# Eight whole gates in place of twelve behind the second mixer of a hybrid decoder step

## The chip, the cores and the metric

The kernel runs on one core of a Trainium2 chip. The metric is the device time of one execution in microseconds (us); the figure for the kernel before is the median of three runs. A core has five engines with instruction streams of their own: TensorE (PE, with its weight loads shown apart as PEld), VectorE (DVE), ScalarE (ACT), GpSimd (POOL) and SyncE (SP, which here only issues transfers). They wait for one another through semaphores. PE multiplies into eight banks of PSUM; everything else lives in SBUF or in memory (HBM).

## What is computed

One step of a decoder layer for a prompt of 512 tokens and eight samples of one token each, so 520 columns in all. The input is normalised and modulated to h, and one wide projection of h feeds two token mixers that run in parallel, a matrix memory (mLSTM) and a forgetting attention (FoX), and the gates that merge them. A gated MLP with a short convolution follows.

```python
mq, mk, mv, mo, mi, mf, fq, fk, fv, ff, ga, gb = jnp.split(h @ w_in + b_in, SPLIT_POINTS, axis=-1)
...
y_m = mlstm_output(h_m, mo, m_hnorm_w)
q_f = rmsnorm(split_heads(fq, F_HEADS), f_qnorm_w)
k_f = rmsnorm(split_heads(fk, F_HEADS), f_knorm_w)
v_f = split_heads(fv, F_HEADS)
lf_f = jax.nn.log_sigmoid(ff.astype(jnp.float32))
y_f = fox_fn(q_f, k_f, v_f, lf_f)
merged = jax.nn.sigmoid(ga) * (y_m @ w_proj_a) + jax.nn.sigmoid(gb) * (y_f @ w_proj_b)
x = x + g1 * (merged @ w_out)
```

The model width is 2048. FoX has 8 heads of 128. For the prompt it is causal attention with a bias from the forget values, swept in blocks of 128 queries. For the samples the past lies in pages of 128 rows, two pages for each of the eight samples, found through a page table; a page row holds all eight heads.

```python
pk = cache_k[layer, page_table].reshape(DB, P, H, Dh).astype(k.dtype)
pv = cache_v[layer, page_table].reshape(DB, P, H, Dh).astype(v.dtype)
...
s = jnp.einsum('bqhd,bkhd->bhqk', q, k_all).astype(jnp.float32) * scale
s = s + (Fq.transpose(0, 2, 1)[..., :, None] - F.transpose(0, 2, 1)[:, :, None, :])
p = jax.nn.softmax(s, axis=-1).astype(v.dtype)
out = jnp.einsum('bhqk,bkhd->bqhd', p, v_all)
```

## The kernel before

**Tiles and precision.** A weight chunk is 128 rows of 2048 values, in two halves of 128x1024. Every product is made of three: ACT casts the half to a high part (`wh`), DVE subtracts to get the low part (`wl`), and PE multiplies high by high, high by low and low by high. An activation has 520 columns, in two pieces of 260, so one 128x128 block of a weight costs 6 matmuls of 260 columns. The inputs `h` lie as pairs of tiles `hh`, `hl`.

**Gates.** Of the 32 gate chunks (16 `ga`, 16 `gb`), `NG` = 2 are made early. `gates = range(NG, KC + NB2)` is made two by two by `GatePair`, in the loop of pairs (`run_pairs`): a unit of 7 steps, each of 24 matmuls, makes two chunks with 7 products in place of 8 (the products are the tiles `x`, `y` and `z`), and the sums that this asks for are DVE work. Pairs whose chunk belongs to `gb` write it to memory (`dsg`), from where it is fetched for the merge. The remaining `range(NB2, KC)` of `gb`, twelve chunks before, are whole gates: 16 blocks of 6 matmuls each in two `halves`, tile `gate`.

**The second mixer behind the gates.** The last loop before the projection `pb` runs over the 24 halves, and each half has 8 steps of 6 matmuls: 192 steps. Behind each step it runs what `plan` holds for that step, put there by hand with `put(step, f)`. PE, DVE, ACT are in program order from the pair loop on, SP and POOL from its end on, so a step's place in the code is its place on every engine, and a waiting instruction holds up all behind it on its engine. In half n, the weights of half n + 4 are loaded at its step 3 (`gate_load`), and those of half n + 2 are cast at step 2 (`gate_cast`, ACT) and split at step 4 (`gate_low`, DVE).

**Heads.** Head hh starts at b = 1 + 22 hh. Its five inputs are loaded at b − 20 (`f_load`); `f_norm` scales q and k (tiles `fi`, DVE); `f_split`, `f_values` and their low parts make `fqh`, `fkh`, `fvh` (ACT) and `fql`, `fkl`, `fvl` (DVE); `f_scores` for four blocks of queries at b + 8, 9, 11, 12 make `fS` (PE), a step later `f_max` adds the bias and takes the maximum (DVE, tile `fs`) and ACT the exponential, two steps on `f_scale` divides (DVE). At b + 19 to 21 `f_turn` transposes the weights into `fPT` (PE), and `f_turn_low`, two steps later, makes `fpl` (DVE), after which that bank is free. `f_attend` follows at b + 26 to 29. The ring of banks `mm_ps`, for all these PSUM tiles, has four.

**Samples.** Sixteen units of key pages (two pages of the table by one half of the heads; `s_load`) each load one query row `qb` to all partitions and gather two tiles `kp` of 128x512 with an indirect transfer that POOL issues. `s_scores` is a multiplication and a reduction for each tile on DVE. Then come the offsets (`s_offsets`, whose product reads the tile `lfd`), the turn of all scores (`s_turn`, tiles `pqk` and `sS`), the maximum, the weights, and eight `s_attend` (tile `sO`) of four value tiles `vp` each. `y_split` and `y_sample` bring the outputs of prompt and samples together for `pb`.

**Rings.** `st` holds 33 tiles, `pt` 9, `raw` (128x1024, weights) 7, `wh` and `wl` 3 each. A tile is free for its next owner once the last reader of the one before is done; the issuing engine waits for that.

Of the kernel before, what the change touches and what calls it, by code (L numbers as in the profile page):

```python
# [22 lines left out]
NS = 8  # L23
# [4 lines left out]
FH = 8  # L28
# [35 lines left out]
def tile_hybrid_step(ctx: ExitStack, tc: tile.TileContext, I, O):  # L64
    nc = tc.nc
    S, V, G, T, Y = nc.scalar, nc.vector, nc.gpsimd, nc.tensor, nc.sync
# [20 lines left out]
    def mconst(shape, name, dt=F32, tag=None):  # L87
        return cm.tile(shape, dt, tag=tag or name, name=name)
# [16 lines left out]
    def dram(shape, name):  # L105
        return dp.tile(shape, F32, tag=nm(name), name=nm(name))
# [48 lines left out]
    def raw_tile():  # L155
        return wp.tile([P, 1024], F32, tag="raw", name=nm("raw"), bufs=7)
# [18 lines left out]
    def on(f, *a):  # L175
        return lambda: f(*a)
# [416 lines left out]
    h = []  # L593
# [42 lines left out]
    T, V, S = (Ordered(tc, e) for e in (T, V, S))  # L636
# [90 lines left out]
    for i, (c0, n) in enumerate(phases):  # L727
        todo = {j: [] for j in range(NPRE)}

        def put(j, f, *a):  # L730
            todo[j].append(on(f, *a))
# [13 lines left out]
        if i + 1 < len(phases):  # L745
            a, b = range(c0 + n, c0 + 2 * n)
# [86 lines left out]
    T, V, S = nc.tensor, nc.vector, nc.scalar  # L833
# [33 lines left out]
    def gather(dst, src, idx):  # L867
        return G.indirect_dma_start(dst, None, src, bass.IndirectOffsetOnAxis(ap=idx, axis=0))
# [9 lines left out]
    acc, gt, _ = w_in("gates")  # L878
# [338 lines left out]
    H = mheads = follows = None  # L1217
# [40 lines left out]
                G.dma_start(dxf[i + 8 * (n == 4)][:, :N], t[:, :N])  # L1258


    NB2 = 4
    assert (NG + NB2) % 2 == 0
    dsg = dram([KC, P, N], "dsg")

# [172 lines left out]
    def s_load(i):  # L1437

        e, b = divmod(i, NS)
        qb = pt("qb")  # L1440
        Y.dma_start(qb[:, :512], dqf[e, b].partition_broadcast(P))
        kps = [pt("kp") for _ in range(NPG)]
        W.k[i] = qb, kps
        for g, kp in enumerate(kps):
            gather(kp[:, :512], I["cache_k"], idx_h[e][:, b * NPG + g:b * NPG + g + 1])

    class Pages:
        pass

    W = Pages()  # L1450
    W.v, W.k = {}, {}

    root = {}
    dss, drr = dram([2, FH, N], "dss"), dram([2, FH, N], "drr")
# [48 lines left out]
    t0, tq = 7 * (len(units) - 2), 7 * (2 * FH)  # L1503
    halves = [(j, e) for j in range(NB2, KC) for e in range(2)]
    gw = {}

    def gate_load(n):
        if n < len(halves):
            j, e = halves[n]
            gw[n] = raw_tile()  # L1510
            Y.dma_start(gw[n], I["w_in"][1 + 24 + 24 + KC + j][:, e * 1024:(e + 1) * 1024])

    def gate_cast(n):
        if n < len(halves):
# [10 lines left out]
    def gate_split(n):  # L1525
        gate_cast(n)
        gate_low(n)

    def upper():
# [6 lines left out]
    late_steps = {7 * (KC + 2): late_turn, tq + 2: root_load, tq + 5: root_make, tq + 8: rows_load, tq + 11: rows_make,  # L1536
                  tq + 15: lambda: (s_rows(0), s_rows(1)), t0 + 9: lambda: (hX.pop(5), f_load(heads[0]), upper()),
                  t0 + 8: lambda: (gate_load(0), gate_load(1)),
                  t0 + 10: lambda: (gate_load(2), gate_load(3)), t0 + 11: lambda: (s_load(0), s_load(1)),
                  t0 + 12: on(gate_split, 0), t0 + 13: lambda: (gate_split(1), f_norm(heads[0]))}  # L1540
    for k in range(KC):
        late_steps.update({7 * (1 + k) + 3: on(late_load, k), 7 * (1 + k) + 6: on(late_product, k)})

# [2 lines left out]
    for j in range(KC):  # L1546
# [11 lines left out]
        if j < NG:  # L1558
            t = sgs[j]
            V.tensor_tensor(z2(t), acc, z2(t), op=ALU.mult)  # L1560
        else:
            t = pt("pao")
# [10 lines left out]
    T, V, S = (Ordered(tc, e) for e in (T, V, S))  # L1573
    for n in (7, 4):
        for i in range(8):
            t = st("hf", F32R)
# [78 lines left out]
    def f_max(H, i):  # L1655
        n = (i + 1) * P
        ps = H.fs.pop(i)
        s = st("fs")
        sm = tiny("sm")
        V.tensor_tensor_reduce(s[:, :n], ps[:, :n], H.nf[:, :n], 1.0, -3e38, ALU.add, ALU.max, sm[:, 0:1])  # L1660
        V.tensor_scalar(sm[:, 0:1], sm[:, 0:1], -1.0, None, op0=ALU.mult)
        S.activation(s[:, :n], s[:, :n], AF.Exp, bias=sm[:, 0:1], accum_out=sm[:, 1:2])
        H.p.append(s)
        H.sm[i] = sm
        if i == NB - 1:
            H.q = H.k = H.v = H.qr = H.kr = H.nf = None
# [34 lines left out]
        S.copy(yf[-1][:, :SEQ], H.y)  # L1701
        H.vt = H.last = H.y = None

    sc = mconst([P, NPG, NS, FH], "sc", tag="m1")
    pp = st("pp")
    yS = mconst([P, NS, FH], "yS")

    def s_scores(i, g):
        e, b = divmod(i, NS)
        qb, kps = W.k[i]  # L1710
        kp = kps[g]
        V.tensor_tensor(kp[:, :512], kp[:, :512], qb[:, :512], op=ALU.mult)
        V.tensor_reduce(sc[:, g, b, e * 4:e * 4 + 4], kp[:, :512].rearrange("p (h d) -> p h d", h=4),
                        axis=AX.X, op=ALU.add)
        if g == NPG - 1:
            del W.k[i]

    def s_bias():
        V.tensor_tensor(sc, sc, sbias, op=ALU.add)
# [39 lines left out]
    def s_gather(i):  # L1759

        e, g, b = i // 8 % 2, i // 4 % 2, i // 16 * 4 + i % 4
        W.v[i] = (pt if i // 4 % 2 else st)("vp")
        gather(W.v[i][:, :512], I["cache_v"], idx_h[e][:, b * NPG + g:b * NPG + g + 1])

    def s_attend(n):
# [40 lines left out]
        S.copy(hi[:, SEQ:N], yS[:, :, hh])  # L1806
        V.tensor_tensor(lo[:, SEQ:N], yS[:, :, hh], hi[:, SEQ:N].bitcast(F32), op=ALU.subtract)

    HP = 22
    for hh, H in enumerate(heads):  # L1810
        b = 1 + hh * HP
        if hh:
            put(b - 20, f_load, H)
            put(b, f_norm, H)
        put(b + 1, f_forget, H)
        put(b + 4, f_keys_out, H)
        put(b + 2, f_split, H)
        put(b + 3, f_values, H)
        put(b + 4, f_split_low, H)
        put(b + 5, f_values_low, H)  # L1820
        for s, i in ((8, 0), (9, 1), (11, 2), (12, 3)):
            put(b + s, f_scores, H, i)
            put(b + s + 1, f_max, H, i)
            put(b + s + 3, f_scale, H, i)
        for j in range(3):
            put(b + 19 + j, f_turn, H, j)
            put(b + 21 + j, f_turn_low, H, j)
        for j in range(NB):
            put(b + 26 + j, f_attend, H, j)
        put(b + 31, f_result, H)  # L1830
        put(max(148 + 4 * hh, b + 31), y_split, hh)
        put(max(148 + 4 * hh, b + 31) + 1, y_low, hh)
    put(3, s_offsets)
    put(5, s_keep)
    for i in range(16):
        if i > 1:
            put(6 + 20 * i // 3, s_load, i)
        put(17 + 20 * i // 3, s_scores, i, 0)
        put(20 + 20 * i // 3, s_scores, i, 1)
    put(126 - 3, s_bias)  # L1840
    put(126, s_turn)
    put(126 + 2, s_max)
    put(126 + 4, s_scale)
    put(126 + 5, s_weights)
    put(126 + 7, s_places)
    for i in range(12):
        put(128 + i, s_gather, i)
    for n in range(8):
        t = 138 + 5 * n
        put(t, s_attend, n)  # L1850
        for i in range(n * 4 + 12, min(n * 4 + 16, 32)):
            put(t + 1 + i % 4 * 5 // 5, s_gather, i)
        if n % 2:
            put(t + 2, s_copy)
            put(t + 7, s_heads, n // 2)
            put(t + 7 + 2, s_add, n // 2)
    for hh in range(FH):
        put(184 if hh < FH - 1 else 188, y_sample, hh)

    H = None  # L1860
    mg = [None] * KC

    def run(fs):
        for f in fs:
            f()

    def fetch_gate(j):
        mg[j] = st("sgm")
# [34 lines left out]
    T, V, S, G, Y = nc.tensor, nc.vector, nc.scalar, nc.gpsimd, nc.sync  # L1903
# [3 lines left out]
    h = None  # L1907
# [165 lines left out]
    for n, j in enumerate(order):  # L2073
# [193 lines left out]
    part = {}  # L2267
# [369 lines left out]
    for k in range(0, KC, 2):  # L2637
        t = 7 * (4 + 2 * k)
# [114 lines left out]
```

## Time and profile before

| | |
|---|---|
| median of three runs | 2860.67 us (2860.51 to 2860.81) |
| the profiled execution | 2849.74 us |
| its span, first to last instruction | 2848.0 us |
| mean granted clock of PE | 0.998 |
| the mixer's stage, first to last gate matmul | 1002.84 to 1203.88 us |

The profile is one execution; its times are from the span's start. Line L60 of the profile is a helper through which the ordered engines record their operations, so that operations are told apart by the tiles that they write and read. A name such as `fS` stands for all tiles of that name, and `x4` counts instructions. PE and PEld overlap: a weight load runs while the matmul before it still does. DVE's time for one instruction overlaps its neighbour's a little, so that busy times of groups sum to more than the engine's busy time.

### The profile page before, as it was taken

What the parts mean: (1) busy time and instruction counts of PE and PEld (TensorE: products, weight loads), DVE (VectorE), ACT (ScalarE), POOL (GpSimd) and SP (SyncE); (2) the same over time, 40 slices, a digit from 0 to 9 for tenths busy, and PEclk for the clock granted to TensorE, in tenths of its full rate; (3) what the DMA queues carried; (4) which work ended last, traced back from release to release, by engine and by line L of the source; (5) the groups of instructions that cost most, each with busy time, mean ns of one, the idle gap of its engine ahead of it and who ended that gap; (6) DMA issues with size and microseconds to landing.
All of it is one profiled execution on the core that took longest, in us unless ns stands there. A gap on an engine that the chain in (4) does not pass through costs nothing.

```text
span 2848.0 us, 57587 instructions
## 1 busy us (share of the span) xinstructions
PE 2821.2 (99%) x23318; PEld 2713.1 (95%) x23318; DVE 2166.4 (76%) x3334; ACT 1360.1 (48%) x2131; POOL 374.7 (13%) x651
## 2 busy tenths in 40 slices
PE   8999999999999999999999999999999999999999
PEld 6888998999999999899999999999999999999999
DVE  5986764676677788478888888787788887788787
ACT  4335553455555444444555444444444445444543
POOL 0001110201100222302211101010010101100100
PEclk9999999999999999999999999999999999999999
DMA  9946657945555577767672434444443346755753
GB/s 338 316 143 202 226 183 258 302 168 180 192 179 184 177 256 243 250 218 228 209 242 83 150 128 140 135 149 145 141 135 128 126 138 188 203 160 167 188 161 104
DMA packets 228036, 531.44 MB, mean 187 GB/s; under 512 B 30305, under 2 KB 83025, under 8 KB 227769
## 3 DMA queue, kind: packets, MB, share of 16 engines
q1 hardware_dynamic: 190176, 432.21, 46.7%
q0 software_dynamic: 37152, 95.31, 11.0%
q8 instruction: 183, 3.00, 0.4%
q14 instruction: 85, 0.69, 0.1%
q10 hardware_dynamic: 440, 0.23, 0.0%
HBM read 451.28 MB, written 72.92 MB: 184 GB/s over the span
## 4 chain that ended last, share of the span: by engine, by line
PE 91%; DVE 4%; ACT 2%; DMA 1%; issue 1%; SPq 0%; POOL 0%; ACTq 0%; DVEq 0%
PE x L60 34%; PE y L60 17%; PE z L60 8%; PE gate L60 5%; PE fo L60 3%; PE pa L213 3%; PE pb L213 3%; PE pre L60 3%; PE mo L213 2%; PE adp L60 2%; PE mv L213 2%; PE adp L409 1%; DVE wl L60 1%; ACT wh L60 1%; PE mq L213 1%
## 5 line engine op out<-in xcount | busy, mean ns | idle before, releaser
L60 DVE TENSOR_TENSOR wl<-raw,wh 128x1024 fp32r<-128x1024 f32 (+1 forms) x690 | 831.6, 1206 | 354.8 <-ACT wh L60 350.5
L60 ACT CAST wh<-raw 128x1024 fp32r<-128x1024 f32 (+1 forms) x690 | 714.5, 1036 | 762.7 <-DVE raw L60 388.8
L60 PE MATMUL x<-bf,wh 128*128 128x260 f32 x2624 | 477.3, 283 | 0.0
L60 DVE TENSOR_TENSOR raw<-raw,raw 128x1024 f32<-128x1024 f32 x339 | 413.8, 1221 | 6.1 <-issue 0.3
L60 PEld LDWEIGHTS x<-bf,wh 128*128 128x128 f32 x2624 | 404.6, 188 | 0.0
L60 PE MATMUL x<-bf,wl 128*128 128x260 f32 x1312 | 370.3, 282 | 0.0
L60 PEld LDWEIGHTS x<-bf,wl 128*128 128x128 f32 x1312 | 247.0, 188 | 0.0
L60 PE MATMUL y<-bf,wh 128*128 128x260 f32 x1312 | 240.2, 283 | 0.0
L60 PEld LDWEIGHTS y<-bf,wh 128*128 128x128 f32 x1312 | 202.1, 189 | 0.0
L60 PE MATMUL x<-ff,wh 128*128 128x260 f32 x1024 | 186.4, 283 | 0.0
L60 PE MATMUL y<-bf,wl 128*128 128x260 f32 x656 | 185.7, 283 | 0.0
L60 PE MATMUL x<-hf,wh 128*128 128x260 f32 x1008 | 185.4, 284 | 0.0
L60 PEld LDWEIGHTS x<-hf,wh 128*128 128x128 f32 x1008 | 154.9, 188 | 13.4 <-DVE tt L60 6.7
L60 PEld LDWEIGHTS x<-ff,wh 128*128 128x128 f32 x1024 | 157.7, 188 | 0.0
L168 DVE TENSOR_TENSOR wl<-raw,wh 128x1024 fp32r<-128x1024 f32 x68 | 83.1, 1223 | 90.0 <-ACT wh L167 89.3
L60 PE MATMUL x<-ff,wl 128*128 128x260 f32 x512 | 144.4, 282 | 0.0
L60 PE MATMUL x<-hf,wl 128*128 128x260 f32 x504 | 142.1, 282 | 0.0
L167 ACT CAST wh<-raw 128x1024 fp32r<-128x1024 f32 x68 | 71.3, 1048 | 134.3 <-DMA raw<-in_w_in 40.0
L60 PE MATMUL fo<-fe,wh 128*128 128x260 f32 x768 | 125.5, 284 | 1.1 <-DVE fo L60 0.9
L60 PEld LDWEIGHTS y<-bf,wl 128*128 128x128 f32 x656 | 123.7, 189 | 0.0
L60 PE MATMUL z<-bf,wh 128*128 128x260 f32 x656 | 120.3, 284 | 0.0
L60 PEld LDWEIGHTS fo<-fe,wh 128*128 128x128 f32 x768 | 105.6, 188 | 2.7 <-DVE fo L60 2.2
(639 smaller groups left out, 7033.7 us busy)
## 6 DMA issues: line engine op xcount, KB each, us to landing
raw<-in_w_fi SPq DMA_DIRECT2D x176, 512.0 KB, 4.0
raw<-in_w_in SPq DMA_DIRECT2D x155, 512.0 KB, 5.7
ar<-in_w_ada SPq DMA_DIRECT2D x192, 256.0 KB, 6.2
raw<-in_w_ada SPq DMA_DIRECT2D x96, 512.0 KB, 4.6
raw<-in_w_fo SPq DMA_DIRECT2D x64, 512.0 KB, 4.0
raw<-in_w_out SPq DMA_DIRECT2D x32, 512.0 KB, 5.1
raw<-in_w_fo SPq DMA_DIRECT2D x32, 384.0 KB, 3.7
dff<-cc POOLq DMA_DIRECT2D x44, 260.0 KB, 4.3
```

What stands on the lines that cost most here:

```text
L60: return lambda *a, **k: self.tc.keep_in_program_order(getattr(self.eng, op)(*a, **k))
L167: S.copy(wh[:, :n], raw[:, :n])
L168: V.tensor_tensor(wl[:, :n], raw[:, :n], wh[:, :n].bitcast(F32), op=ALU.subtract)
L213: T.matmul(acc[:, z, :HN], a[:, o], b[:, z * HN:(z + 1) * HN], start=(k == 0 and i == 0), stop=(k == K - 1 and i == 2))
L409: ins = T.matmul(ps[32 * g:32 * g + 32, :], cs[:, k, :], w, start=first, stop=last, tile_position=(0, 32 * g))
```

## The change

`NB2` goes from 4 to 8: four more gate chunks are made in pairs (two more units, 23 in all), and eight whole gates in 16 halves, 128 steps, stand where twelve stood. The plan of the second mixer is fitted to the 128 steps:

- a head every 13 steps (`HP`), its loads 13 steps ahead;
- key units 0 to 3 in the last steps of the pair loop (loads at the pair steps 133, 140, 147 and 152, scores from 143, 150, 157 and 162), unit 4 loaded there; units 4 to 15 scored every 5.5 steps from step 8 on. From unit 5 (`PT`) on both tiles of a unit lie in one tile of the ring `raw`, and one multiplication and one reduction over 1024 values do what two of each did;
- the score turn at step 74 instead of 126, value gathers from step 74 on, the attends at 83 + 5n instead of 138 + 5n, all value tiles in the ring `pt`: eight gathers ahead, then four behind each attend, where twelve were ahead and half of the tiles lay in `st`;
- `f_max` takes the minimum of the negated sum, so that the operation that turned the sign of the maximum goes.

```diff
-    NB2 = 4
+    NB2 = 8
...
-        kps = [pt("kp") for _ in range(NPG)]
+        kps = [pt("kp")[:, :512] for _ in range(NPG)] if i < PT else raw_tile().rearrange("p (g n) -> p g n", g=NPG)
         W.k[i] = qb, kps
-        for g, kp in enumerate(kps):
-            gather(kp[:, :512], I["cache_k"], idx_h[e][:, b * NPG + g:b * NPG + g + 1])
+        for g in range(NPG):
+            gather(kps[g] if i < PT else kps[:, g], I["cache_k"], idx_h[e][:, b * NPG + g:b * NPG + g + 1])
+
+    PT = 5
...
+        elif part == 0:
+            V.tensor_tensor(kps, kps, qb[:, :512].unsqueeze(1).to_broadcast([P, NPG, 512]), op=ALU.mult)
+        else:
+            V.tensor_reduce(sc[:, :, b, e * 4:e * 4 + 4], kps.rearrange("p g (h d) -> p g h d", h=4),
+                            axis=AX.X, op=ALU.add)
...
-                  t0 + 10: lambda: (gate_load(2), gate_load(3)), t0 + 11: lambda: (s_load(0), s_load(1)),
-                  t0 + 12: on(gate_split, 0), t0 + 13: lambda: (gate_split(1), f_norm(heads[0]))}
+                  t0 + 10: lambda: (gate_load(2), gate_load(3)), t0 + 12: on(s_load, 4),
+                  t0 + 11: on(gate_split, 0), t0 + 13: lambda: (gate_split(1), f_norm(heads[0]))}
+    late_steps = {t: [f] for t, f in late_steps.items()}
+    pages = ((133, 143), (140, 150), (147, 157), (152, 162))
+    for i, (a, b) in enumerate(pages):
+        for t, f in ((a, on(s_load, i)), (b, on(s_scores, i, 0)), (b + 2, on(s_scores, i, 1))):
+            late_steps.setdefault(t, []).append(f)
...
-        V.tensor_tensor_reduce(s[:, :n], ps[:, :n], H.nf[:, :n], 1.0, -3e38, ALU.add, ALU.max, sm[:, 0:1])
-        V.tensor_scalar(sm[:, 0:1], sm[:, 0:1], -1.0, None, op0=ALU.mult)
-        S.activation(s[:, :n], s[:, :n], AF.Exp, bias=sm[:, 0:1], accum_out=sm[:, 1:2])
+        V.tensor_tensor_reduce(s[:, :n], ps[:, :n], H.nf[:, :n], -1.0, 3e38, ALU.add, ALU.min, sm[:, 0:1])
+        S.activation(s[:, :n], s[:, :n], AF.Exp, bias=sm[:, 0:1], scale=-1.0, accum_out=sm[:, 1:2])
...
-        W.v[i] = (pt if i // 4 % 2 else st)("vp")
+        W.v[i] = pt("vp")
...
-    HP = 22
+    HP = 13
...
-            put(b - 20, f_load, H)
+            put(b - 13, f_load, H)
...
-        put(max(148 + 4 * hh, b + 31), y_split, hh)
-        put(max(148 + 4 * hh, b + 31) + 1, y_low, hh)
+        put(max(96 + 4 * hh, b + 31), y_split, hh)
+        put(max(96 + 4 * hh, b + 31) + 1, y_low, hh)
...
+    for i in range(4, 16):
+        b = 8 + 11 * (i - 4) // 2
+        if b > 11:
+            put(b - 11, s_load, i)
+        put(b, s_scores, i, 0)
+        put(b + 2, s_scores, i, 1)
+    put(71, s_bias)
+    put(74, s_turn)
+    put(76, s_max)
+    put(78, s_scale)
+    put(79, s_weights)
+    put(81, s_places)
+    for i in range(8):
+        put(74 + i, s_gather, i)
     for n in range(8):
-        t = 138 + 5 * n
+        t = 83 + 5 * n
         put(t, s_attend, n)
-        for i in range(n * 4 + 12, min(n * 4 + 16, 32)):
+        for i in range(n * 4 + 8, min(n * 4 + 12, 32)):
             put(t + 1 + i % 4 * 5 // 5, s_gather, i)
         if n % 2:
             put(t + 2, s_copy)
-            put(t + 7, s_heads, n // 2)
-            put(t + 7 + 2, s_add, n // 2)
+            put(t + 4, s_heads, n // 2)
+            put(t + 6, s_add, n // 2)
     for hh in range(FH):
-        put(184 if hh < FH - 1 else 188, y_sample, hh)
+        put(125 if hh < FH - 1 else 127, y_sample, hh)
```

Where a middle head's turns meet the next head's scores, PE's order before is as follows: two transposes of the last turn (`fPT` from the weights `fs`), two steps of gate matmuls (`hh`, `hl` are the inputs, `wh`, `wl` the weights), and then the next head's forget row (`nFb`).

```order
L60 MATMUL fPT_12723<-ident,fs_12612 128x128
L60 MATMUL fPT_12723<-ident,fs_12630 128x128
L60 MATMUL gate_12546<-hh_1954,wh_12472 128x260 x2
L60 MATMUL gate_12546<-hl_1955,wh_12472 128x260 x2
L60 MATMUL gate_12546<-hh_1954,wl_12473 128x260 x2
L60 MATMUL gate_12546<-hh_2174,wh_12472 128x260 x2
L60 MATMUL gate_12546<-hl_2175,wh_12472 128x260 x2
L60 MATMUL gate_12546<-hh_2174,wl_12473 128x260 x2
L60 MATMUL nFb_12745<-rows_2657,sel 128x512
```

The same place on PE after the change:

```order
L60 MATMUL fPT_13179<-ident,fs_13022 128x128
L60 MATMUL fPT_13179<-ident,fs_13044 128x128
L60 MATMUL fS_13185<-fi_12835,fi_12834 128x128
L60 LDWEIGHTS identb
L60 MATMUL fS_13185<-mask_f,identb 128x128
L60 MATMUL gate_13125<-hh_857,wh_12896 128x260 x2
L60 MATMUL gate_13125<-hl_858,wh_12896 128x260 x2
L60 MATMUL gate_13125<-hh_857,wl_12897 128x260 x2
L60 MATMUL fS_13207<-fkh_13090,fqh_13087 128x256
L60 MATMUL fS_13207<-fkl_13091,fqh_13087 128x256
L60 MATMUL fS_13207<-fkh_13090,fql_13088 128x256
```

The first scores of the next head (`fS`) have moved right behind the last transposes of this one, with one step of gates before the second scores; its forget row and splits lie further up.

On DVE the low parts of the turns (`fpl`) come before the next head's norms (`fi`), splits (`fql`, `fkl`, `fvl`) and pages (`kp`, `sc`):

```order
L60 TENSOR_TENSOR fpl_12694<-fPT_12688,fph_12693 128x512
L60 TENSOR_TENSOR fpl_12710<-fPT_12704,fph_12709 128x384
L60 SCALAR_TENSOR_TENSOR fi_12456<-fi_12456,qwc,fi_12458 128x520
L60 SCALAR_TENSOR_TENSOR fi_12457<-fi_12457,nkw,fi_12459 128x520
L60 TENSOR_TENSOR fpl_12727<-fPT_12723,fph_12726 128x256
L60 TENSOR_TENSOR kp_12568<-kp_12568,qb_12565 128x512
L60 TENSOR_REDUCE sc<-kp_12568 128x4
L60 TENSOR_TENSOR fql_12764<-fi_12456,fqh_12763 128x512
L60 TENSOR_TENSOR fkl_12767<-fi_12457,fkh_12766 128x512
L60 TENSOR_TENSOR fvl_12792<-vtp_12786,fvh_12791 128x384
L60 TENSOR_TENSOR kp_12661<-kp_12661,qb_12659 128x512
L60 TENSOR_REDUCE sc<-kp_12661 128x4
```

After the change the same operations of DVE stand in this order (an ISA row is the bias and maximum of `f_max`, and the page tiles are now `raw` of 128x1024):

```order
L60 TENSOR_TENSOR fql_13088<-fi_12834,fqh_13087 128x512
L60 TENSOR_TENSOR fkl_13091<-fi_12835,fkh_13090 128x512
L60 TENSOR_TENSOR fvl_13106<-vtp_13100,fvh_13105 128x384
L60 TENSOR_REDUCE sc<-raw_12914 128x2x4
L60 TENSOR_TENSOR fpl_13150<-fPT_13144,fph_13149 128x512
L60 TENSOR_TENSOR raw_12995<-raw_12995,qb_12993 128x1024
L60 TENSOR_TENSOR wl_13159<-raw_12908,wh_13158 128x1024
L60 TENSOR_TENSOR fpl_13167<-fPT_13161,fph_13166 128x384
L60 ISA fs_13203,sm_13204<-fS_13185,nfb_13074 128x128
L60 ISA sm_13204 128x1
L60 TENSOR_TENSOR fpl_13183<-fPT_13179,fph_13182 128x256
L60 ISA fs_13219,sm_13220<-fS_13207,nfb_13074 128x256
```

The next head's splits have moved ahead of this head's turns, a page's multiplication and a weight's split stand between two of them, and the next head's first maximum comes before the last.

More of the change, by code (lines that the diff above doesn't have):

```diff
@@ L1451, in tile_hybrid_step, with s_scores, run @@
     W.v, W.k = {}, {}
+    sc = mconst([P, NPG, NS, FH], "sc", tag="m1")
+    def s_scores(i, part):
+        e, b = divmod(i, NS)
+        qb, kps = W.k[i]
+        if i < PT:
+            V.tensor_tensor(kps[part], kps[part], qb[:, :512], op=ALU.mult)
+            V.tensor_reduce(sc[:, part, b, e * 4:e * 4 + 4], kps[part].rearrange("p (h d) -> p h d", h=4),
+                            axis=AX.X, op=ALU.add)
[3 more added lines that the diff above has]
+            V.tensor_reduce(sc[:, :, b, e * 4:e * 4 + 4], kps.rearrange("p g (h d) -> p g h d", h=4),
+                            axis=AX.X, op=ALU.add)
+        if part == NPG - 1:
+            del W.k[i]
+    def run(fs):
+        for f in fs:
+            f()
     root = {}
@@ L1538, in tile_hybrid_step @@
                   t0 + 8: lambda: (gate_load(0), gate_load(1)),
-                  t0 + 10: lambda: (gate_load(2), gate_load(3)), t0 + 11: lambda: (s_load(0), s_load(1)),
-                  t0 + 12: on(gate_split, 0), t0 + 13: lambda: (gate_split(1), f_norm(heads[0]))}
+                  t0 + 10: lambda: (gate_load(2), gate_load(3)), t0 + 12: on(s_load, 4),
[5 more added lines that the diff above has]
+            late_steps.setdefault(t, []).append(f)
+    late_steps = {t: on(run, f) for t, f in late_steps.items()}
     for k in range(KC):
@@ L1702, in f_result @@
         H.vt = H.last = H.y = None
-    sc = mconst([P, NPG, NS, FH], "sc", tag="m1")
     pp = st("pp")
     yS = mconst([P, NS, FH], "yS")
[L1708 to L1716, printed above, removed]
     def s_bias():
@@ L1830, in tile_hybrid_step @@
         put(b + 31, f_result, H)
-        put(max(148 + 4 * hh, b + 31), y_split, hh)
-        put(max(148 + 4 * hh, b + 31) + 1, y_low, hh)
+        put(max(96 + 4 * hh, b + 31), y_split, hh)
+        put(max(96 + 4 * hh, b + 31) + 1, y_low, hh)
     put(3, s_offsets)
     put(5, s_keep)
[L1835 to L1847, printed above, removed]
+    for i in range(4, 16):
[12 more added lines that the diff above has]
+        put(74 + i, s_gather, i)
     for n in range(8):
-        t = 138 + 5 * n
+        t = 83 + 5 * n
         put(t, s_attend, n)
-        for i in range(n * 4 + 12, min(n * 4 + 16, 32)):
+        for i in range(n * 4 + 8, min(n * 4 + 12, 32)):
             put(t + 1 + i % 4 * 5 // 5, s_gather, i)
@@ L1854, in tile_hybrid_step @@
             put(t + 2, s_copy)
-            put(t + 7, s_heads, n // 2)
-            put(t + 7 + 2, s_add, n // 2)
+            put(t + 4, s_heads, n // 2)
+            put(t + 6, s_add, n // 2)
     for hh in range(FH):
-        put(184 if hh < FH - 1 else 188, y_sample, hh)
+        put(125 if hh < FH - 1 else 127, y_sample, hh)
     H = None
     mg = [None] * KC
-    def run(fs):
-        for f in fs:
-            f()
     def fetch_gate(j):
```

## The prediction

> **What bounds the kernel now.** The page's first part and its chain of waits come first: is there one engine to which everything is owed?
>
> ```profile
> PE 2821.2 (99%) x23318; PEld 2713.1 (95%) x23318; DVE 2166.4 (76%) x3334; ACT 1360.1 (48%) x2131; POOL 374.7 (13%) x651
> PE 91%; DVE 4%; ACT 2%; DMA 1%; issue 1%; SPq 0%; POOL 0%; ACTq 0%; DVEq 0%
> ```
>
> There is: PE works 99% of the span and holds 91% of the chain. A change pays only by taking matmuls off PE, and costs only where it lets PE wait. DVE's 76% is a mean over stages, so the table of busy time by stretch comes next: some 42 us of the pair loop, the whole stage of the second mixer (first to last gate matmul), three of its heads exactly (between the same matmul of one head and of the third after it), a stretch of the stage behind it, and the stretch of the attends.
>
> ```profile
> 955.00:997.00 42.00, 42.00 (x354) 42.00 (x353) 31.43 (x33) 19.96 (x29) 10.39 (x14) 1.00 0.56 188
> 1002.84:1203.88 201.04, 200.09 (x1580) 184.79 (x1578) 149.55 (x356) 96.45 (x206) 64.29 (x65) 1.00 0.74 247
> 1028.61:1093.66 65.05, 65.05 (x522) 62.93 (x521) 60.81 (x133) 32.23 (x68) 20.24 (x20) 1.00 0.81 269
> 1240.00:1300.00 60.00, 60.00 (x502) 60.00 (x501) 48.63 (x80) 27.10 (x44) 10.12 (x19) 1.00 0.61 187
> 1140.00:1190.00 50.00, 50.00 (x383) 39.77 (x381) 27.24 (x78) 22.52 (x48) 26.48 (x26) 1.00 0.80 294
> ```
>
> After the stretch and its length stand busy time (and instructions) of PE, PE's weight loads, DVE, ACT and POOL, then the granted clock, the DMA share and GB/s. While heads and key pages run, DVE is busy 60.81 of 65.05 us, against 31.43 of 42.00 in the pair loop. PE never waits there, yet a schedule that shortens PE's part of this stage and keeps DVE's presses on an engine with 6.5% left.
>
> **The change part by part.** *PE's work.* Four whole gates of 96 matmuls go, 384; two pairs of 168 come, 336. All are 260 columns wide. The bare stretch gives 60.00 / 502 = 0.1195 us for one; two units of the pair loop lie between these starts:
>
> ```profile
> 956.91 0.28 PE L60 MATMUL z<-hh,wh 128*128 128x260 f32 x1
> 997.10 0.28 PE L60 MATMUL z<-hh,wh 128*128 128x260 f32 x1
> ```
>
> 40.19 us for 336, the same 0.1196. So the balance is 48 × 0.1195 = **−5.7 us**. The Trainium skill, "TensorE: Matmul & The Clock Gate", section "Back-to-back issue gap", gives N/2.4 + 2.5 ns for an isolated warm matmul, 111 ns at 260 columns, and says that weight loads change the spacing of a real stream; by the formula the balance would be an estimated −5.3 us. The rows have 119.5 ns, and the measurement decides.
>
> *PE's two old stalls.* In the stage PE is idle 201.04 − 200.09 = 0.95 us by the table, at the score turn; one attend also takes 2.04 us where others take 1.06, waiting for a value page:
>
> ```profile
> 1129.46 0.28 PE L60 MATMUL sS<-ones,pqk 128*64 128x1 f32 x2 [0.95 <-DVE pqk L60]
> 1148.33 2.04 PE L60 MATMUL sO<-vp,pp 128*32 128x512 f32 x8
> 1155.53 1.06 PE L60 MATMUL sO<-vp,pp 128*32 128x512 f32 x8
> ```
>
> That is 0.95 + 0.98 = **−1.9 us** if nothing takes their place; I book new ones apart.
>
> *DVE against PE in the new keys stage.* A head every 13 steps instead of 22, a page every 5.5 steps instead of 6.67. DVE's groups in the three-head stretch:
>
> ```profile
> L60 DVE TENSOR_REDUCE sc<-kp 128x4 f32<-128x512 f32 x20 | 13.7, 686 | 0.7
> L60 DVE TENSOR_TENSOR kp<-kp,qb 128x512 f32<-128x512 f32 x20 | 13.7, 684 | 0.0
> L60 DVE TENSOR_TENSOR wl<-raw,wh 128x1024 fp32r<-128x1024 f32 x8 | 9.7, 1218 | 0.0
> L60 DVE CUSTOM_DVE_ANT_0 fs<-fS,nfb 128x128 f32<-128x128 f32 (+3 forms) x12 | 5.8, 487 | 2.4 <-PE fS L60 2.4
> L60 DVE TENSOR_TENSOR fpl<-fPT,fph 128x256 fp32r<-128x256 f32 (+2 forms) x10 | 5.2, 536 | 0.0
> L60 DVE TENSOR_SCALAR fs<-fs,sm 128x128 f32<-128x128 f32 (+3 forms) x12 | 4.8, 400 | 0.4
> L60 DVE SCALAR_TENSOR_TENSOR fi<-fi,nkw,fi 128x520 f32<-128x520 f32 x3 | 2.3, 753 | 0.0
> L60 DVE SCALAR_TENSOR_TENSOR fi<-fi,qwc,fi 128x520 f32<-128x520 f32 x3 | 2.3, 750 | 0.0
> L60 DVE TENSOR_TENSOR fkl<-fi,fkh 128x512 fp32r<-128x512 f32 x3 | 2.1, 685 | 0.0
> L60 DVE TENSOR_TENSOR fql<-fi,fqh 128x512 fp32r<-128x512 f32 x3 | 2.0, 682 | 0.0
> L60 DVE RECIPROCAL sm<-sm 128x1 f32<-128x1 f32 x12 | 2.0, 163 | 0.3 <-ACT fs L60 0.3
> L60 DVE TENSOR_SCALAR sm<-sm 128x1 f32<-128x1 f32 x12 | 1.8, 154 | 0.4
> L60 DVE TENSOR_TENSOR fvl<-vtp,fvh 128x384 fp32r<-128x384 f32 x3 | 1.7, 550 | 0.0
> L60 DVE DVE_READ_ACCUMULATOR2_ANT sm<- 128x1 f32 x12 | 1.0, 83 | 0.0
> ```
>
> They sum to 68.1 us against 60.81 busy: neighbours overlap by 7.3 / 133 = 0.055 us each. In after, three heads take 39 steps. PE: 66 steps of before hold 66 × 6 × 0.1195 = 47.3 us of gate matmuls and so 17.7 of head matmuls; 39 steps are 28.0 + 17.7 = **45.7 us**. DVE: heads 68.1 − 13.7 − 13.7 − 9.7 = 31.0, less 1.8 for the sign operation that the change drops and 0.4 for a tenth turn that belongs to a neighbouring head, = 28.8; 39/8 weight halves × 1.218 = 5.9; 39/5.5 = 7.1 pages. A fused page costs one multiplication and one reduction of 1024. The multiplication is like the split of the same shape, 1.22. The reduction isn't in the trace: at least the 0.69 of half its width, at most two of these, 1.37; I take 1.22, since 512 more elements add 1.218 − 0.684 = 0.53 to its neighbour. Pages: 7.1 × 2.44 = 17.3. Sum 52.0, with 91 instructions 52.0 − 91 × 0.055 = **47.0 us** (43.2 to 48.1 by the ends). DVE thus falls 1.3 us behind in 39 steps. It can't be carried far: the PE rows of the change show the next head's first scores right behind the turns of the head before, into the bank that DVE's low half of the turn (fpl) frees. In before six steps of gates lie between; after, PE waits there for DVE once a head. The last head whose scores meet page work is the fifth, so 65 steps count: 1.3 × 65/39 = 2.2 us.
>
> DVE's own idle comes on top. Before, 65.05 − 60.81 = 4.2 us in three heads, 1.4 each, mostly waiting for fS (2.4 in the row of the scores). If DVE is behind, the scores are there when it gets to them: 0. If it keeps all: 5 × 1.4 = 7. I take a quarter, 1.8, since a late engine seldom waits. Together **+4.0 us** (0 to 11).
>
> *Edges of the stage.* Page 3 is scored at the last pair steps, and DVE's lfd stands behind it; the offsets at step 3 wait for that: 0 to 1.4 (two reductions), I take 0.5. The score turn still asks for DVE's pqk with no lead, 0 to 0.95: 0.5, since pages end a few steps sooner. The tail has outputs of the samples two steps before the end; PE then goes into the next products behind a DVE subtraction: 0 to 1, I take nothing, for DVE is 27.24 of 50.00 busy in the attends' stretch.
>
> *Values.* All 32 pages now go through the ring of nine, four gathers behind each attend for the attend two on:
>
> ```profile
> L60 POOL DMA_INDIRECT vp<-in_cache_v,idx x32: 945/949/1823, 1118.5 to 1173.0; - x32
> DMA to landing us min/median/max: 3.8/6.4/9.5
> 1142.15 1.06 PE L60 MATMUL sO<-vp,pp 128*32 128x512 f32 x8
> 1186.62 1.06 PE L60 MATMUL sO<-vp,pp 128*32 128x512 f32 x8
> ```
>
> Eight attends start 1142.15 to 1186.62, 6.35 us apart, so ten steps give 12.7 us. An attend's 1.06, four gathers at 0.95 and a median landing of 6.4 make 11.3: in time, by 1.4. With the longest landing 14.4: late by 1.7. I take **+1.0** over six attends (0 to 10).
>
> *Covered edits.* Two more pairs lengthen the loop; DVE has 10.6 of 42 us free there, and the four early pages cost it 4 × 2.74 = 11 us over some three units (60 us): hidden. ACT's four sigmoids fewer lie in the merge, where ACT waits for DVE and PE: nothing. The dropped sign operations are counted above. SP's transfers: the stage's DMA share rises from 0.81 by the ratio of steps; PE stood no stall at 0.80 to 0.81.
>
> **Sum**, against the profiled run of 2849.74 us: −5.7 − 1.9 + 4.0 + 0.5 + 0.5 + 1.0 = **−1.6**, 2848.1. The median of the timed runs lies 10.93 above that run, so 2860.67 − 1.6 = **2859.1 us**. This kernel's measurement tells 0.2%, 5.7 us, from no change; the forecast lies inside.
>
> **The rivals.** *DVE keeps pace.* A reduction of 1024 at 0.9, or fewer idle gaps, leaves no new stall in the stage: −7.6 + 1 = −6.6, **2854.1**. For it: the sums differ by 3% only. Against: the bank has no slack.
>
> *DVE keeps its idle.* All 1.4 per head: 7 + 2.2 instead of 4.0, **2864.2**. For it: each head's exponentials on ACT stand between two DVE operations. Against: the denser stream of pages fills such gaps.
>
> *The ring of nine (slower side).* At step t+1 behind each attend POOL begins the four gathers that the attend at t+10 needs; it is slower from a landing of 12.7 − 1.06 − 3.8 = 7.8 us, against a median of 6.4 and a maximum of 9.5, at 294 GB/s. With every later group at 9.5, six attends wait 1.7: +10.2 in place of 1.0, **2868.3**. For it: even before, one attend waited 0.98. Against: the median. The Trainium skill, "SBUF — State Buffer", section "Who interferes with whom", says that DVE's tensor_scalar can lock GpSimd out of a shared port pair while it writes descriptors; with heads 13 steps apart that would speak against the change. The gathers' median of 949 ns, 945 at least, beside DVE's scaling of 400 ns shows hardly a trace of it, and the maximum of 1823 one case.
>
> *The pair loop stalls.* With six page tiles in the ring of nine, a pair's temporaries wait for the write of the pair before; at two or three microseconds in three units, some 7 on top: **2866.1**. Nothing in before shows it.
>
> **How the numbers follow.** Forecast 0.44 (2855 to 2863), DVE keeps pace 0.24, keeps its idle 0.13, ring 0.13, pair loop 0.06. Faster by over 0.2% is below 2854.9: the first rival, 0.24. Within 0.2%, up to 2866.4: forecast, idle and half the pair loop, 0.60. Slower: 0.16. Range: 2853.0 (no stall anywhere is 2853.1) to 2867.5, where most of the ring case falls out.
>
> **What would show it.** 384 fewer gate and 336 more pair matmuls; the stage shorter by some 42 us (46 of gates less new stalls) and the loop longer by 40. PE idle before fS, released by DVE fpl, of 2 to 6 us between steps 9 and 74, DVE over 95% busy there: right. No such idle: the first rival. PE's weight loads waiting for vp: the ring. ACT's or DVE's pair temporaries waiting for dsg, with PE idle before x, y or z in the last three units: the pair loop. The forecast is wrong if a 1024 reduction is far from 1.22, or if stages that the change doesn't touch move.

## The result, and the profile after

| | before | after | ratio (95% interval) |
|---|---|---|---|
| median | 2857.51 us (2852.54 to 2861.22) | 2847.05 us (2844.14 to 2851.42) | 0.9966 (0.9956 to 0.9977) |
| profiled execution, span | 2849.74, 2848.0 | 2846.27, 2844.6 | |

The kernel became faster by 0.34%, some 9.7 us. (Five more runs of before brought its median from 2860.67 to 2857.51 us.) The forecast was −1.6 us with a range down to 2853.0; the result is below the range and on the faster side, to which the prediction gave 0.24. The two profiled executions differ by less, 3.4 us of span, because that of before lay 7.8 us under its median.

Where the time went is read first from two tiles that bracket the stages. The rows give, for a product, the start of its first and last matmul; `z<-hh` opens the loop of pairs, `pb<-yfl` comes at the end of the mixer's stage, and `z<-bf` spans a loop of the gated MLP that the change doesn't touch. Before:

```profile
L60 PE MATMUL z<-bf,wh x656: 279/283/388, 1550.9 to 2376.9; 128*128 128x260 f32 x164
L60 PE MATMUL z<-hh,wh x168: 279/282/286, 568.0 to 999.6; 128*128 128x260 f32 x168
L213 PE MATMUL pb<-yfl,wh x256: 277/283/288, 1204.2 to 1295.9; 128*128 128x260 f32 x128
```

The same three of the changed kernel:

```profile
L60 PE MATMUL z<-bf,wh x656: 277/283/390, 1552.2 to 2373.2; 128*128 128x260 f32 x164
L60 PE MATMUL z<-hh,wh x184: 279/282/286, 568.9 to 1040.8; 128*128 128x260 f32 x184
L213 PE MATMUL pb<-yfl,wh x256: 277/283/287, 1206.0 to 1297.7; 128*128 128x260 f32 x128
```

From the first z<-hh to the first pb<-yfl, the region that the prediction's sum is about, it takes 1204.2 − 568.0 = 636.2 us before and 637.1 after: 0.9 us *more*. The loop of bf takes 826.0 us before and 821.0 after: 5.0 less, though neither its work nor its order was changed. So what these two traces show as a gain lies in a place that the prediction left out.

In the stage itself the changed kernel's PE shows these waits (start, duration, what, and in brackets the idle time ahead of it with what ended it):

```profile
1047.92 0.43 PE L60 MATMUL sbias<-lfd,ones 8*128 8x64 f32 x2 [0.18 <-DVE lfd L60]
1071.09 0.39 PE L60 MATMUL fS<-fkh,fqh 128*128 128x256 f32 x1 [2.19 <-DVE fpl L60]
1117.29 0.39 PE L60 MATMUL fS<-fkh,fqh 128*128 128x256 f32 x1 [0.31 <-DVE fpl L60]
1150.99 0.49 PE L60 MATMUL fS<-fi,fi 128*128 128x128 f32 x2 [1.63 <-issue]
1153.93 0.39 PE L60 MATMUL fS<-fkh,fqh 128*128 128x256 f32 x1 [1.61 <-DVE fpl L60]
```

The wait for the bank that fpl frees is there, as predicted, and neither pqk nor a value page is waited for. The keys stage in the table by stretch, and DVE's page rows in it:

```profile
1054.00:1114.00 60.00, 57.60 (x451) 54.48 (x450) 57.48 (x118) 33.20 (x78) 25.45 (x23) 1.00 0.90 302
1064.00:1084.00 20.00, 17.60 (x138) 16.45 (x137) 19.82 (x38) 11.13 (x27) 6.48 (x6) 1.00 0.93 299
```

```profile
L60 DVE TENSOR_TENSOR raw<-raw,qb 128x1024 f32<-128x1024 f32 x9 | 11.0, 1218 | 0.0
L60 DVE TENSOR_REDUCE sc<-raw 128x8 f32<-128x1024 f32 x8 | 9.7, 1211 | 0.0
```

DVE is busy 57.48 of 60 us, and 19.82 of the 20 in which PE waits 2.4. The reduction of 1024, which the prediction put at 1.22 us, took 1.211. The waits near 1151 are not of this kind: from 1140 to 1156 DVE is busy for only 6.88 us of 16.

### The profile page after: what moved, and what is told of

Read it like the earlier page. It is cut to its first block, busy times and chain, and to the rows that moved or that the text cites. A ratio compares the mean times of both kernels' runs of the same rounds, so it can differ in the third digit from the quotient of the medians.

```text
span 2844.6 us, 57501 instructions
## 1 busy us (share of the span) xinstructions
PE 2811.4 (99%) x23270; PEld 2702.7 (95%) x23270; DVE 2173.1 (76%) x3300; ACT 1364.8 (48%) x2143; POOL 382.2 (13%) x659
## 4 chain that ended last, share of the span: by engine, by line
PE 89%; DMA 4%; DVE 4%; ACT 1%; issue 1%; SPq 0%; POOL 0%; DVEq 0%; ACTq 0%; POOLq 0%
PE x L60 34%; PE y L60 17%; PE z L60 9%; PE fo L60 4%; PE pa L213 3%; PE pb L213 3%; PE gate L60 2%; PE mo L213 2%; PE pre L60 2%; DMA ar<-in_w_ada 2%; PE mv L213 2%; PE adp L60 2%; PE adp L409 1%; DVE wl L60 1%; PE mq L213 1%
## 5 line engine op out<-in xcount | busy, mean ns | idle before, releaser
L60 DVE TENSOR_TENSOR raw<-raw,raw 128x1024 f32<-128x1024 f32 x347 | 423.5, 1220 | 6.2 <-issue 0.3
L60 PE MATMUL x<-hf,wh 128*128 128x260 f32 x1104 | 203.0, 284 | 0.0
L60 PEld LDWEIGHTS x<-hf,wh 128*128 128x128 f32 x1104 | 169.7, 188 | 13.4 <-DVE tt L60 6.7
L60 PE MATMUL x<-hf,wl 128*128 128x260 f32 x552 | 155.7, 282 | 0.0
```

The source lines that it names most:

```text
L60: return lambda *a, **k: self.tc.keep_in_program_order(getattr(self.eng, op)(*a, **k))
```

## The experiments

### Twice the same kernel, a step more of lead, and no page work

The first two runs change nothing. The third moves each head's scores, with their maxima, a step later:

```diff
-        for s, i in ((8, 0), (9, 1), (11, 2), (12, 3)):
+        for s, i in ((9, 0), (10, 1), (12, 2), (13, 3)):
```

The fourth cuts the scores of units 5 to 15 to four columns and leaves the rest of those products out:

```diff
-            V.tensor_tensor(kps, kps, qb[:, :512].unsqueeze(1).to_broadcast([P, NPG, 512]), op=ALU.mult)
+            V.tensor_tensor(kps[:, :, :4], kps[:, :, :4], qb[:, :4].unsqueeze(1).to_broadcast([P, NPG, 4]), op=ALU.mult)
...
-            V.tensor_reduce(sc[:, :, b, e * 4:e * 4 + 4], kps.rearrange("p g (h d) -> p g h d", h=4),
-                            axis=AX.X, op=ALU.add)
+            V.tensor_copy(sc[:, :, b, e * 4:e * 4 + 4], kps[:, :, :4])
```

> The kernel before, unchanged, profiled a second time, to see which part of the difference between the two traces belongs to the kernel. Of the two traces at hand the mixer's region (from the first z of the pair loop to the first product behind pb) is 0.8 us longer after the change, and a loop that the change doesn't touch, the products of bf between 1540 and 2375 us, is 5.0 us shorter: 0.1201 us for a matmul before, 0.1194 after. If the pace of that loop belongs to the kernel (theory: the change shifts which buffers and PSUM banks the loop's tiles get), this profile shows 0.1201 again. If it differs from execution to execution (rival), it shows anything between 0.119 and 0.121, and the span moves with it by up to 5 us. PE should show the two stalls of before again, 0.95 us at pqk and about 1 us at one attend.

> The changed kernel, unchanged, profiled a second time. If the pace belongs to the kernel, 0.1194 again in the bf loop and a time of 0.996 to 0.998 of before; if it is chance, the loop's pace differs from the first profile and the ratio comes nearer to 1. The stalls of PE before fS (2.2 us near 1071, 1.6 and 1.6 us near 1151) should stand at the same places if they come from the order of the program; if they come from the moment's traffic, they move.

> The change with each head's four scores, maxima and divisions one step later, so that one step of gate matmuls (0.72 us) stands between a head's turns and the next head's first scores. My theory, that PE waits for the bank which DVE's fpl frees because it asks for it without any lead: PE's idle before fS falls from about 5.7 us to 2 or 3, the time by 2 to 4 us against the change. Rival, DVE has no time left in the keys stage (57.5 of 60 us busy): the wait only moves by a step, the sum of idle stays 5 to 7 us, the time within 1 us of the change.

> The change with the scores of key units 5 to 15 cut to four columns of each page (their loads stay; the multiplications and reductions over the rest, and so right scores for these pages, are left out): DVE gets some 11 x 2.4 = 26 us back in the keys stage. If DVE's load sets PE's stalls there, PE's idle before fS falls to under 1 us near 1071, and the time by 3 to 6 us; the stalls near 1151, behind the last page, stay or go with the lead that DVE has. If the traffic sets them (the loads are all there), they stay.

All four ran on one chip, beside a before of 2850.64 us. Region and loop are the two lengths defined above.

| | median us | ratio to before | region | loop of bf |
|---|---|---|---|---|
| e1, before | 2850.29 | 1.0000 (0.9991 to 1.0009) | 636.9 | 825.9 |
| e2, the change | 2841.64 | 0.9965 (0.9952 to 0.9979) | 631.5 | 821.0 |
| e3, scores later | 2838.75 | 0.9957 (0.9943 to 0.9970) | 631.2 | 820.2 |
| e4, short scores | 2840.97 | 0.9967 (0.9955 to 0.9979) | 629.2 | 824.1 |

The loop's length belongs to the program: 826.0 and 825.9 in two profiles of before, 821.0 and 821.0 in two of the change. The region doesn't: the change needs 637.1 us in its first profile and 631.5 here. The rows of the region for e1 and then e2:

```profile
L60 PE MATMUL z<-hh,wh x168: 279/282/286, 567.4 to 999.4; 128*128 128x260 f32 x168
L213 PE MATMUL pb<-yfl,wh x256: 277/283/288, 1204.3 to 1296.0; 128*128 128x260 f32 x128
L60 PE MATMUL z<-hh,wh x184: 279/282/286, 569.3 to 1041.1; 128*128 128x260 f32 x184
L213 PE MATMUL pb<-yfl,wh x256: 277/283/287, 1200.8 to 1292.5; 128*128 128x260 f32 x128
```

In e2 PE waits less, and the two waits near 1151 are gone:

```profile
1048.28 0.43 PE L60 MATMUL sbias<-lfd,ones 8*128 8x64 f32 x2 [0.17 <-DVE lfd L60]
1070.19 0.38 PE L60 MATMUL fS<-fkh,fqh 128*128 128x256 f32 x1 [1.35 <-DVE fpl L60]
1116.39 0.39 PE L60 MATMUL fS<-fkh,fqh 128*128 128x256 f32 x1 [0.34 <-DVE fpl L60]
```

What made the waits near 1151 in the first profile is seen on ACT, which must cast a head's turns before DVE can free the bank. In the first profile of the change PE's four transposes start at 1146.67, and the cast behind them three microseconds later:

```profile
1146.67 0.60 PE L60 MATMUL fPT<-ident,fs 128*128 128x128 f32 x4
1149.63 0.58 ACT L60 CAST fph<-fPT 128x512 fp32r<-128x512 f32 x1 [4.38 <-PE fPT L60]
```

In e2 it follows at once:

```profile
1145.74 0.60 PE L60 MATMUL fPT<-ident,fs 128*128 128x128 f32 x4
1146.38 0.59 ACT L60 CAST fph<-fPT 128x512 fp32r<-128x512 f32 x1 [2.04 <-PE fPT L60]
```

So PE's signal came late: the cast starts 2.4 us behind the end of the transposes (1146.67 + 0.60 to 1149.63), against 0.04 us in e2. In the trace's record of semaphores, 34 of PE's signals in that profile have no entry within half a microsecond of their matmul's end, all between 1043 and 1189 us; in e1 to e4 and in the first profile of before every signal has one, 14 ns behind the end in the median. The 34 are not all late signals, for some entries are missing altogether, of DVE and ACT too; that signals were late is told by the engines that waited, as ACT did here. On this chip, then, the region can be compared without them: 631.5 − 636.9 = −5.4 us. e4, where DVE has time, gives 629.2 − 636.9 = −7.7: that is the prediction's −5.7 − 1.9 = −7.6 for PE's work and its two old stalls, so those terms stand within the 0.7 us by which two profiles of before differ (636.2 and 636.9), and DVE's load costs 2.3 us of the region, not 4.0 or more. e4's PE has one wait left in the stage, 0.19 us for lfd. The time of e4 is no lower than e2's nevertheless, since its loop of bf is 3.1 us longer. e3 gained 0.3 us in the region, as the rival said (its waits before fS are 0.86 and 0.48 us): with DVE full, a step of lead only shifts the wait. Its 2.9 us come mostly from elsewhere, 0.8 of them from the loop.

### What sets the pace of the loop that nobody touched

In e4 and the change, PE's instructions ahead of the loop are the same, and so are the banks of PSUM that the loop uses; the buffers of the ring `st` that its moving operands get are not, for a ring's tiles go to whichever buffer is free. Two runs of *before* tell buffers from banks. Each takes one idle tile behind the gates, e5 from `st`, e8 from PSUM:

```diff
+    spare = st("spare")
+    G.memset(spare[:, :1], 0.0)
+    spare = None
```

```diff
+    for i in range(1):
+        spare = mm_ps("spare")
+        V.memset(spare[:, :1], 0.0)
+    spare = None
```

e6 is the change with the tile of e5. In e7 the pages are unfused again:

```diff
-            V.tensor_tensor(kps, kps, qb[:, :512].unsqueeze(1).to_broadcast([P, NPG, 512]), op=ALU.mult)
+            for g in range(NPG):
+                V.tensor_tensor(kps[:, g], kps[:, g], qb[:, :512], op=ALU.mult)
...
-            V.tensor_reduce(sc[:, :, b, e * 4:e * 4 + 4], kps.rearrange("p g (h d) -> p g h d", h=4),
-                            axis=AX.X, op=ALU.add)
+            for g in range(NPG):
+                V.tensor_reduce(sc[:, g, b, e * 4:e * 4 + 4], kps[:, g].rearrange("p (h d) -> p h d", h=4),
+                                axis=AX.X, op=ALU.add)
```

> The kernel before, with one more tile of the ring st taken and set to zero in one column by POOL right behind the gates, which is no work on anybody's path but makes later tiles of that ring get other buffers; the banks of PSUM stay. Theory: the pace of the bf loop, 20.167 us for a unit in two profiles of before and 20.040 in two of the change, hangs on such placement and not on what the change does: the unit's time leaves 20.167 by 0.02 to 0.2 us, for all units alike, and the span moves by 1 to 6 us either way, most of it between 1540 and 2375 us. Rival, the pace comes from something that the change itself does: 20.167 again and the time within 1 us of before.

> The change with the same idle tile. Theory: a unit of the bf loop leaves 20.040 us, likely towards a longer one (20.01 and 20.11 are what the two variants had), with a time 0 to 6 us above the change's; rival: 20.040 and the same time. The mixer's stage isn't touched and should keep PE's three waits, 1.35, 0.34 and 0.17 us.

> The change with two multiplications and two reductions of 512 for each key unit again in place of one of 1024 each. By the rows a unit costs DVE 2.74 us less overlap instead of 2.43: 11 units give 2.4 to 3.4 us more DVE work between steps 8 and 74, where DVE is 58.3 of 60 us busy. If DVE has no time left there, PE's waits before fS grow from 1.7 to 4 us or more and the stage with them; if DVE's idle takes it up, they stay under 2.5 us. The time is read from the stage, since the bf loop may get another pace.

> The kernel before, with one more PSUM bank taken and set to zero in one column by DVE behind the gates: in the bf loop y and z then lie in other banks (5, 6 and 7, 4 instead of 4, 6 and 7, 5), while every tile of the ring st keeps its buffer. If banks set the loop's pace, the unit leaves 20.167 us; if they don't and the buffers of st do, it stays at 20.167 and the time within 1 us of before.

These ran on another chip, beside a before of 2857.14 us.

| | median us | ratio to before | region | loop of bf |
|---|---|---|---|---|
| e5, before, other buffers | 2855.14 | 0.9981 (0.9969 to 0.9992) | 640.8 | 820.9 |
| e6, change, other buffers | 2850.29 | 0.9970 (0.9958 to 0.9983) | 637.0 | 822.9 |
| e7, unfused | 2848.55 | 0.9961 (0.9945 to 0.9976) | 639.7 | 821.3 |
| e8, before, other banks | 2857.83 | 0.9998 (0.9986 to 1.0009) | 647.0 | 826.0 |

e5 has the work of before and the loop of the change: 820.9 us. e8 has other banks and the loop of before, 826.0; of its 168 matmuls a unit every one keeps its pitch (the time to the next matmul's start, in the mean over the units) to 0.1 ns, and of e5's, 107 get one that is over a nanosecond off, by up to 10 ns. The same 700 us of the loop, in before, e2, e5 and e8, in this order (PE's matmuls in the second bracket of numbers):

```profile
1600.00:2300.00 700.00, 700.00 (x5827) 687.40 (x5826) 560.79 (x685) 319.78 (x408) 76.17 (x170) 1.00 0.43 140
```

```profile
1600.00:2300.00 700.00, 700.00 (x5862) 687.38 (x5862) 563.16 (x688) 321.19 (x412) 76.23 (x170) 1.00 0.44 140
```

```profile
1600.00:2300.00 700.00, 700.00 (x5862) 687.39 (x5861) 562.42 (x687) 321.45 (x410) 76.86 (x170) 1.00 0.44 141
```

```profile
1600.00:2300.00 700.00, 700.00 (x5827) 687.40 (x5826) 559.93 (x679) 319.31 (x407) 76.82 (x170) 1.00 0.44 139
```

PE is never idle in any, the granted clock is 1.00 in all, DMA the same; 5827 or 5862 matmuls fit, by the buffers of that ring alone. This is the cause of the 5.0 us, and it is no property of the change: one idle tile gave it to before, and the same idle tile took 1.9 of it from the change (e6). How an address acts on the pitch stays open: the same tile at the same address has another pitch in another program, so that no single buffer is slow. The idle tile shifts the ring's other tiles too, which DVE and ACT work on, and no run tells these from the moving operands.

e7 against e6 was to price the fusion: 639.7 − 637.0 = 2.7 us of the region, within the 2.4 to 3.4 us of DVE work that the unfused pages add. The sum misleads. From the first gate matmul to the score turn (the first sS that reads pqk), where the pages are scored, e7 takes 89.2 us (1043.8 to 1133.0) and e6 88.1 (1043.6 to 1131.7): 1.1 us more. The rest lies behind the turn, in a wait near 1153 that grew from 1.6 to 3.0 us, and in the clock of PE behind that wait, 0.66 of full speed against 1.00 in e6 (the first number behind the fifth bracket; e7 first):

```profile
1154.00:1159.00 5.00, 4.79 (x26) 2.71 (x25) 2.41 (x10) 2.99 (x8) 0.96 (x1) 0.66 0.92 356
1154.00:1159.00 5.00, 5.00 (x38) 3.62 (x38) 2.78 (x9) 2.91 (x8) 2.85 (x3) 1.00 0.90 307
```

So the fusion is worth 1.1 us as far as these traces show it, less than was expected. e7's median is below e6's all the same, the loop again (1.6 us) and what else differs from execution to execution.

Late signals are back on this chip, in all four profiles, those of before too: by the count above, 31 to 41 in each. They aren't alone. The trace records when PE was granted half its clock, and in the region that happened for 3.4 us in e5, 3.4 in e7 and 10.2 in e8, where matmuls of 260 columns start 215 to 219 ns apart in the median instead of some 119; in e1 to e4, e6 and the first profiles of before and of the change it didn't happen there. Each such stretch begins during a wait of PE or within 1.7 us of the end of one; not every wait has one behind it. e8's region is 10 us longer than e1's by its waits (8.2 us against 1.2 in the stage) and this clock together. The granted clock goes with the time in the unchanged kernel too: of the 26 runs of before on this chip, the eight with a mean clock of 0.998 or more took 2852.5 to 2857.3 us, the ten with 0.996 or less 2859.6 to 2866.8. That the 10.93 us by which the first profile of before lay under the median of its three runs are of this kind is likely and not shown, since no trace of those runs is kept.

### A better schedule

> The change with scores a step later (as in e3) and one more key unit, the fourth, loaded and scored in the pair loop; the other eleven stand 6 steps apart from step 9 on. DVE loses 2.7 us of work between steps 8 and 74. Theory (DVE's load makes PE's last waits in the stage): PE's waits before fS, 1.34 us in e3, fall under 0.5 us and the stage from the first gate matmul to the first whole product of pb gets 1 to 2 us shorter than e3's. Rival: the unit's work in the pair loop is late for the offsets (PE waits for lfd 1 us or more instead of 0.19), and nothing is won. The bf loop may get another pace, so that the stage is compared, not the time.

> The changed kernel once more, as the measure for the two beside it on the same chip: 0.9955 to 0.998 of before, 20.040 us for a unit of the bf loop.

> The kernel of e3 once more beside the change on the same chip: if its gain of 2.9 us belongs to the kernel, 1.5 to 4 us below the change again, with 20.013 us for a unit of the bf loop; its stage should be 0.5 to 1 us shorter than the change's.

e9's edit, on top of e3:

```diff
-                  t0 + 10: lambda: (gate_load(2), gate_load(3)), t0 + 12: on(s_load, 4),
+                  t0 + 10: lambda: (gate_load(2), gate_load(3)), 
...
-    pages = ((133, 143), (140, 150), (147, 157), (152, 162))
+    pages = ((133, 143), (140, 150), (147, 155), (152, 158), (157, 163))
...
-    for i in range(4, 16):
-        b = 8 + 11 * (i - 4) // 2
-        if b > 11:
-            put(b - 11, s_load, i)
+    for i in range(5, 16):
+        b = 9 + 6 * (i - 5)
+        put(max(0, b - 12), s_load, i)
...
-    put(71, s_bias)
+    put(72, s_bias)
```

A third chip, beside a before of 2860.80 us:

| | median us | ratio to before | region | loop of bf |
|---|---|---|---|---|
| e9, a page early | 2853.16 | 0.9972 (0.9963 to 0.9982) | 640.1 | 824.5 |
| e10, the change | 2848.03 | 0.9958 (0.9944 to 0.9971) | 640.7 | 821.0 |
| e11, scores later | 2842.02 | 0.9934 (0.9920 to 0.9947) | 633.6 | 820.1 |

e11 is below the change on both chips where the two ran side by side, by 2.9 and 6.0 us, and is the best of these kernels. Its loop keeps the length of e3, its region is 7.1 us shorter than e10's here. Only half of that is the step of lead. e10 ran 10.2 us of its region at half the clock and e11 none; the first profile of the same changed kernel, with late signals too, ran none either and took 637.1 us, 3.6 less than e10, though it waited no less (6.7 us in the stage against 6.2). One of the two places, in e10 and then in that first profile:

```profile
1152.00:1160.00 8.00, 6.46 (x30) 4.22 (x30) 2.42 (x10) 3.51 (x9) 2.36 (x3) 0.57 0.83 315
1152.00:1160.00 8.00, 6.39 (x47) 4.75 (x46) 4.14 (x13) 4.15 (x11) 2.85 (x3) 1.00 0.88 332
```

PE is busy as long in both, and starts 30 matmuls in one and 47 in the other. Against that first profile, e11's region is 3.5 us shorter and its waits are 3.3 us instead of 6.7: where signals come late the step of lead pays some 3.5 us, by one profile on each of two chips. Whether it also keeps the half clock away is not shown.

e9 missed: PE found a new place to wait, the turns, which now ask for weights that DVE hasn't divided yet, and another ahead of the stage, where the early page's work holds up a pair's sums:

```profile
1042.43 0.47 PE L60 MATMUL x<-hf,wh 128*128 128x260 f32 x2 [1.17 <-DVE tt L60]
1068.62 0.33 PE L60 MATMUL fPT<-ident,fs 128*128 128x128 f32 x1 [2.19 <-DVE fs L60]
1123.57 0.38 PE L60 MATMUL fS<-fkh,fqh 128*128 128x256 f32 x1 [1.06 <-DVE fpl L60]
```

It isn't the wait for lfd that the rival named (0.17 us), but the outcome is the rival's, nothing won; late signals and 3.4 us at half the clock, from 1069 on, blur how much of it is the schedule.

## Why the prediction was wrong

**The step that failed** is the last condition of the prediction, that stages which the change doesn't touch keep their time. The sum had no term for them, and one moved by −5.0 us, in every profile of the change. It is about half of the gain where both halves can be measured, on the first chip of the experiments (−5.4 in the region, −4.9 in the loop, and 1.9 us lost ahead of both, where the first z<-hh starts at 569.3 instead of 567.4, the two ends of that start's range over all profiles); with it alone the forecast of −1.6 would have been −6.6.

**PE's work, −5.7, and the old stalls, −1.9:** right. e4, which has little else, measured −7.7 together.

**DVE against PE, +4.0:** the engine and the wait were right (fS waits for fpl, DVE 58 of 60 us busy, the reduction 1.21 us), and the size too high: 2.3 us by e2 against e4. The load was estimated well. From the second head's first scores to the fifth's, the 39 steps of the prediction, e2 and then e4 show:

```profile
1067.63:1114.84 47.21, 45.86 (x360) 43.56 (x359) 46.38 (x93) 26.41 (x61) 19.40 (x17) 1.00 0.91 309
1067.12:1112.71 45.59, 45.59 (x360) 43.49 (x359) 32.68 (x92) 26.48 (x61) 16.02 (x16) 1.00 0.94 321
```

PE alone needs 45.59 us (predicted 45.7), and DVE is busy for 46.38 (47.0) and idle for 0.83, so that three heads lose 1.6 us where the prediction's two parts make 1.3 and three times a quarter of 1.4. And the wait doesn't come once a head: it stands at the second scores of the second head (1.35 us) and of the fifth (0.34), and the two heads between have none. Charging the loss over 65 steps, head after head, made it too large; the recorded waits before fS, 1.7 us, lie under the 2 to 6 us that the prediction named as its sign.

**Edges, +1.0:** 0.17 us for lfd and none at the score turn.

**Values, +1.0:** none. Landings were 3.2 to 8.6 us in e2, and PE waited for no page; the ring of nine is no bound. The pair loop didn't stall either.

So where no signal is late the region gained 5.4 us and not 1.6, since 2.2 us of waits came in place of 6.0; where they are late it took 637 us without half clock (the first profile of the change, e6) and 641 with 10.2 us of it (e10), against 641 and 647 for before with 3.4 and 10.2 us (e5, e8). Why PE's signals come late in some profiles and not in others, and what brings the half clock, stays open: DMA is as busy at the same place in e2 (375 GB/s between 1140 and 1156) as in the first profile (368), so traffic alone isn't it. No experiment was made on it.

## What to carry to other kernels

When a kernel runs gapless on one engine, compare the stages that a change doesn't touch before explaining the stages that it does; an edit of allocations moves buffers everywhere behind it, and here that was worth 5 us of 2850 with no work changed. A gain under that size isn't the schedule's until an idle allocation has been tried on both kernels. With DVE at 97% beside a full PE, a handshake without lead cost only 2 us, but lateness lands on it: the step of lead that gained 0.3 us of the region where signals were on time gained some 3.5 where they were late. Before two executions are compared, look where each was granted less than the full clock: here that made half of a difference of 7.1 us between two regions.

## What the runs showed of the hardware

In the loop of bf the pitch of matmuls of one shape with nothing idle and the granted clock at 1.00 ranged from 114 to 127 ns by place in the unit (but for the places where a unit ends), the same in every unit and, for one program, in each profile, and its mean over the loop hung on which buffers the tiles of one ring had, moving operands among them: 820.1 to 826.0 us for the same matmuls. PSUM banks had no part in it (826.0 in before and e8). PE's signal reached ACT 2.4 us behind the matmul's end at the place shown, in some profiles only. PE was granted half its clock for 3.4 to 10.2 us of the region in e5, e7, e8, e9 and e10, with matmuls of 260 columns 215 to 219 ns apart; these stretches began in or within 1.7 us of its waits.
